# A hybrid decoder block whose POOL opens with a maximum over partitions, and whose norm scale moves behind the first diagonals

## The chip, the cores and the metric

The kernel runs on one core of one Trainium2 chip. The metric is the device time of one execution, in microseconds (us), as the median of several runs; lower is better. The engines are called as the profile calls them: PE (matrix multiplications; PEld is its weight load), DVE (vector), ACT (activations), POOL (general purpose) and SP (here it only issues DMA transfers).

## The reference, cut to what matters

One decoder block over 1024 tokens of width 1024. The input is normalised over its width and multiplied by the norm weight, one wide projection makes all heads and gates, a linear recurrence (HGRN2) and a sliding-window attention run beside each other, and two output projections follow.

```python
def rms_norm(x, w):
    xf = x.astype(jnp.float32)
    xf = xf * lax.rsqrt(jnp.mean(xf * xf, axis=-1, keepdims=True) + EPS)
    return xf.astype(x.dtype) * w
...
xn = rms_norm(x, norm_w[l])
proj = xn @ w_in[l]
hq, hf, hi, hg, aq, ak, av, ag, mh, ma = jnp.split(proj, SPLIT_POINTS, axis=-1)
lb = lb_all[l]
f = lb + (1.0 - lb) * jax.nn.sigmoid(hf.astype(jnp.float32))
...
merged = jax.nn.sigmoid(mh) * y_h + jax.nn.sigmoid(ma) * y_a
x = x + merged @ w_out[l]
return rms_norm(x, final_norm_w)
```

The change touches the first two lines of the second part: the norm, and the first columns of the projection (`hf`).

## The kernel before

Float32 products are made of float16 ones: each operand is scaled by a power of two and split into a high and a low half, and three products (high by high, high by low, low by high) are summed. So each weight block of 1024 by 256 needs its largest absolute value (DVE reduces each partition, POOL takes the maximum over partitions with `all_max`, L119), a power of two made of it (`pow2_of`, L124, four small DVE operations), a high half on ACT (`hi_part`, L193) and a low half on DVE (`lo_part`, L198). The first weight block is loaded and converted in two parts of 128 columns.

The activations go the same way. Tokens come in tiles of 128. For a tile, ACT squares the row and sums it (`square`, L418) and takes the root of the mean plus `eps` (L419); DVE makes the reciprocal root more exact in four steps and writes it into a diagonal matrix `dg` made from the identity `ident` (`diag`, L430 to L445). PE multiplies the tile by the diagonal, which turns and normalises it at once (`turn_x`, L451, into a bank `xT`, one bank for each 128 columns k, tile j filling a quarter of it). When the four tiles of a half are in a bank, ACT writes the high half `xh` with the scale `nws` (`split_x`, L455) and DVE the low half `xl` (L456). `nws` is the norm weight times a power of two, which comes from the largest norm weight (`norm_max`, L341, and `norm_scale`, L346). PE then multiplies `xh` and `xl` by the first weight block (`mm_first`, L1097, into `pf`).

Until the end of L1190 the order on PE, DVE, ACT and POOL is written out by hand, line by line; each engine works through its own list in order. SP issues its transfers in program order. Behind that a scheduler orders the work.

The lists at the start are, before the change. POOL: memsets of `ident`, `ones` and `eps`, the affine select that makes `ident` a unit matrix (in the helper file masks.py), then the maxima over partitions. PE: four transposes of `ident` into a bank that nobody reads (`warm`, L1091), the norm weight turned from 8 rows into 8 columns (`turn_rows`, L147), twenty more `warm`, then the first `turn_x`. DVE: a copy of the turned norm weight, its maximum, the power of two and `nws` as soon as POOL has answered, then the maximum of the first weight part, its power of two, and only then the diagonals. ACT: a first small Sqrt that reads `eps` (`tab`, L1088), the squares of tiles 0 and 1, `hi_part`, the squares of tiles 2 and 3.

## Time and profile before

| what | value |
|---|---|
| time, median of 3 runs | 1214.54 us (1213.32 to 1217.31) |
| the profiled execution's own time | 1214.3 us |
| its span | 1212.5 us |
| PE busy | 1165.0 us, 96% of the span |
| DVE busy | 832.6 us, 69% |
| ACT busy | 546.9 us, 45% |
| POOL busy | 43.9 us, 4% |

A timeline row gives the start, the duration, the engine, the line with the operation, the tiles written and read, the count of instructions merged into the row, and in brackets the idle time of that engine just before and what ended it. "issue" there means that the engine waited for nothing that the profile shows. In the chain of work that ended last, each row is a start, a length and what ran. [...]

### The profile page before, as it was taken

To read this page: it belongs to the slowest core of one execution; us is meant where nothing else is said; L and a number is where in the kernel's file an instruction comes from. 1 tells how busy PE (TensorE), PEld (TensorE's weight loads), DVE (VectorE), ACT (ScalarE), POOL (GpSimd) and SP (SyncE) were. 2 spreads that over 40 slices of the span, in tenths; PEclk is the share of its full clock that TensorE was granted. 3 is DMA by queue.
4 is the path that set the end of the run, shared out by engine and by line. 5 is a ranking of instruction groups with operands and counts; after the bars stand their busy time and mean duration, and the time that the engine had idled before them with its cause. 6 is when DMAs were issued, how large, how long until landed. Compare 5 with 4: busy or idle time off the path is not lost.

```text
span 1212.5 us, 18364 instructions
## 1 busy us (share of the span) xinstructions
PE 1165.0 (96%) x7258; PEld 689.1 (57%) x7258; DVE 832.6 (69%) x1999; ACT 546.9 (45%) x1053; POOL 43.9 (4%) x97
## 2 busy tenths in 40 slices
PE   4999999999999999999999989999897999999997
PEld 3557687687687667675554544445454444444444
DVE  2876955866686778666787774358896877467645
ACT  2733524444353333525864762138677550223323
POOL 0250000000000000000000000000000000000000
PEclk8999999999999999999999999999999999999999
DMA  5121111111111111111453551114455412121312
GB/s 208 36 96 44 35 36 36 35 36 36 35 36 36 35 36 35 36 36 35 108 105 93 113 114 59 55 39 114 106 108 99 111 35 70 35 96 44 139 53 105
DMA packets 132647, 82.48 MB, mean 68 GB/s; under 512 B 81200, under 2 KB 129360, under 8 KB 132560
## 3 DMA queue, kind: packets, MB, share of 16 engines
q1 hardware_dynamic: 132560, 81.30, 24.4%
q8 instruction: 57, 0.93, 0.3%
q14 instruction: 30, 0.25, 0.1%
HBM read 57.17 MB, written 4.19 MB: 51 GB/s over the span
## 4 chain that ended last, share of the span: by engine, by line
PE 77%; DVE 10%; ACT 6%; DMA 5%; issue 2%; SPq 0%; POOL 0%; DVEq 0%; POOLq 0%; ACTq 0%
PE pm L302 19%; PE pg L302 10%; PE pv L314 7%; PE po L1250 7%; PE pq L302 7%; PE paq L302 5%; PE pf L302 5%; PE lv L582 4%; DMA pT<-ph 3%; ACT sp L784 2%; DVE ph L795 2%; PE pk L302 2%; PE pf L1097 1%; DVE sp L774 1%; DMA aot<-ohl 1%
## 5 line engine op out<-in xcount | busy, mean ns | idle before, releaser
L302 PEld LDWEIGHTS <-wh 128*128 128x128 f16 x2304 | 224.3, 98 | 251.4 <-issue 6.2
L302 PEld LDWEIGHTS <-wl 128*128 128x128 f16 x1152 | 112.8, 98 | 129.4
L235 ACT ACTIVATE wh<-raw,p_s 128x512 f16<-128x512 f32 x164 | 104.8, 709 | 119.9 <-issue 42.7
L236 DVE SCALAR_TENSOR_TENSOR wl<-raw,p_s,wh 128x512 f16<-128x512 f32 x164 | 114.2, 749 | 48.5 <-PE pm L302 18.4
L204 DVE TENSOR_REDUCE wmx<-raw 128x1 f32<-128x2048 f32 x45 | 102.7, 2283 | 63.4 <-DMA raw<-in_w_in_dram 42.5
L302 PE MATMUL pm<-hl,wh 128*128 128x512 f16 x512 | 117.0, 379 | 0.0
L1250 PE MATMUL po<-wo,hl 128*128 128x512 f16 (+1 forms) x408 | 83.1, 366 | 0.0
L784 ACT ACTIVATE sp<-sp,anm 128x256 f32<-128x256 f32 (+1 forms) x128 | 61.7, 483 | 25.1 <-DVE anm L779 24.6
L314 PEld LDWEIGHTS <-xh 128*128 128x128 f16 x640 | 62.7, 98 | 7.6
L1250 PEld LDWEIGHTS <-hl 128*128 128x128 f16 x408 | 39.9, 98 | 43.3
L302 PE MATMUL pg<-xh,wh 128*128 128x512 f16 x256 | 60.8, 379 | 0.9 <-DVE qs L731 0.9
L302 PE MATMUL pg<-xl,wh 128*128 128x512 f16 x256 | 61.6, 379 | 0.0
L587 DVE COPY_PREDICATED sc<-lmask,lv 128x512 f32<-128x512 uint8 x56 | 49.5, 886 | 17.6 <-PE lv L582 17.4
L302 PE MATMUL pm<-xh,wh 128*128 128x512 f16 x256 | 61.3, 381 | 0.0
L302 PE MATMUL pm<-xl,wh 128*128 128x512 f16 x256 | 61.3, 379 | 0.0
L302 PE MATMUL pg<-xh,wl 128*128 128x512 f16 x256 | 61.1, 379 | 0.0
L302 PE MATMUL pm<-xh,wl 128*128 128x512 f16 x256 | 60.6, 379 | 0.0
L302 PE MATMUL pm<-hl,wl 128*128 128x512 f16 x256 | 60.5, 379 | 0.0
L582 PEld LDWEIGHTS lv<-kq 128*128 128x128 f32 x448 | 56.6, 192 | 5.0
L582 PE MATMUL lv<-kq 128*128 128x128 f32 x448 | 58.2, 275 | 0.0
L774 DVE CUSTOM_DVE_ANT_0 sp<-as,amask,qsc 128x256 f32<-128x256 f32 (+1 forms) x128 | 52.3, 463 | 4.5 <-DMA pT<-ph 4.2
L567 ACT ACTIVATE kq<-k 128x512 f32<-128x512 f32 x56 | 35.8, 641 | 42.5 <-PE lv L582 37.8
(209 smaller groups left out, 1879.6 us busy)
## 6 DMA issues: line engine op xcount, KB each, us to landing
raw<-in_w_in_dram SPq DMA_DIRECT2D x33, 1024.0 KB, 5.1
xt<-in_x_dram SPq DMA_DIRECT2D x8, 512.0 KB, 6.7
raw<-in_w_branch_hgrn_dram SPq DMA_DIRECT2D x4, 1024.0 KB, 5.2
raw<-in_w_branch_attn_dram SPq DMA_DIRECT2D x4, 1024.0 KB, 5.4
raw<-in_w_out_dram SPq DMA_DIRECT2D x4, 1024.0 KB, 5.1
xr<-in_x_dram SPq DMA_DIRECT2D x8, 512.0 KB, 7.9
out_dram<-xr SPq DMA_DIRECT2D x8, 512.0 KB, 2.6
raw<-in_w_in_dram SPq DMA_DIRECT2D x2, 512.0 KB, 4.1
```

The lines of the kernel that those rows point to most:

```text
L204: V.tensor_reduce(mx[:, j : j + 1], self.raw[:, ks], axis=AX.XY, op=ALU.max, apply_absolute_value=True)
L235: A.activation(hi, raw, AF.Copy, scale=s[:])
L236: V.scalar_tensor_tensor(lo, raw, s[:], hi, ALU.mult, ALU.subtract)
L302: PE.matmul(ps, w[:, k, ci * P : (ci + 1) * P], act(ai, k, t0, HALF), start=(n == 0), stop=(n == 3 * KT - 1))
L314: PE.matmul(ps, act(ai, k, t0, P), w[:, k, n0 : n0 + ncol], start=(n == 0), stop=(n == 3 * KT - 1))
L567: A.activation(view(kq[:, 0], 0, mdims), view(k, 0, kdims), AF.Copy)
L582: PE.matmul(lv[:, ms], kq[:, 0, ms], kq[:, 1, ms], start=True, stop=True)
L587: V.copy_predicated(view(sc, c, qdims), view(lmask[c], 0, mdims), view(lv, 0, mdims))
L774: V.tensor_tensor_reduce(self.s[:, i, 0:nk], self.ps[a][:, e * 256 : e * 256 + nk], amask[:, self.n % 2, 0:nk], qsc[:], NEG, ALU.add, ALU. ...
L784: A.activation(self.s[:, i, 0 : self.nk], self.s[:, i, 0 : self.nk], AF.Exp, bias=self.nm[:, i : i + 1], accum_out=self.dn[:, i : i + 1],)
L795: V.scalar_tensor_tensor(self.hl[:, 1], self.s[:, :, 0 : self.nk], 2.0**14, self.hl[:, 0], ALU.mult, ALU.subtract)
L1250: PE.matmul(ps[:, g[0] : g[1]], mact(ai, k, tb * P, P), w, start=(t == 0), stop=(t == 3 * KT - 1))
```

## The change

Five things are changed.

1. POOL begins with a memset of a new tile `zero` and a maximum over partitions of it, whose result nobody reads. The affine select on `ident`, and the memsets of `ones` and `eps`, come behind it.
2. The norm weight is loaded by ACT's DMA queue in place of SP's, into 8 rows of a tile of 128 rows that DVE has filled with zeros. Its maximum is taken from these rows, before they are turned.
3. On DVE the diagonals of tiles 0 and 1 come ahead of both powers of two. The power of two of the weight part now comes ahead of that of the norm weight; the turned norm weight is copied only there.
4. The 24 `warm` instructions read a tile `wsrc` that DVE fills with ones, and are plain matrix products in place of transposes; the turning of the norm weight comes behind all of them.
5. The diagonal of tile 2 comes ahead of the low half of the weight part's first rows.

```diff
@@ -132,13 +132,19 @@
+    zero = const.tile([P, 1], F32, name="zero")
+    G.memset(zero[:], 0.0)
+    all_max(zero[:])
     ident = const.tile([P, P], F32, name="ident")
     make_identity(nc, ident[:])
...
-    nwr = slot("nwr", [KT, P])
-    SP.dma_start(nwr[:], norm_w[0].rearrange("(k p) -> k p", p=P))
+    nwr = slot("nwr", [P, P])
+    V.memset(nwr[:], 0.0)
+    A.dma_start(nwr[0:KT, :], norm_w[0].rearrange("(k p) -> k p", p=P))
+    wsrc = slot("wsrc", [P, P])
+    V.memset(wsrc[:], 1.0)
...
@@ -340,12 +346,12 @@
     def norm_max():
         nmx = small("nmx", 1)
-        V.tensor_reduce(nmx[:], nw[:], axis=AX.X, op=ALU.max, apply_absolute_value=True)
+        V.tensor_reduce(nmx[:], nwr[:], axis=AX.X, op=ALU.max, apply_absolute_value=True)
         return all_max(nmx[:])
 
-    def norm_scale(top):
+    def norm_scale(top, turned):
         sx, sxi = pow2_of(top, 10)
-        yield
+        V.tensor_copy(nw[:], turned[:, 0:KT])
         V.tensor_copy(sxi_c[:], sxi[:])
         V.tensor_scalar(nws[:], nw[:], sx[:], None, ALU.mult)
 
@@ -1088,9 +1094,7 @@
         for i in range(WARM):
-            PE.transpose(warm[:, 0:P], ident[:], ident[:])
-            if i == 3:
-                V.tensor_copy(nw[:], turn_rows(nwr, KT)[:, 0:KT])
+            PE.matmul(warm[:, 0:P], wsrc[:], wsrc[:], start=True, stop=True)
...
@@ -1111,19 +1115,20 @@
         hf_tiles(0)
         top = norm_max()
-        in_turn(norm_scale(top))
         first.max_part(0)
         tok[0].square(True)
         tok[1].square(True)
+        in_turn(tok[0].diag())
+        turned = turn_rows(nwr[0:KT], KT)
+        in_turn(tok[1].diag())
         first.scale_part(0)
         first.hi_part(0, 0)
-        in_turn(tok[0].diag())
+        norm_scale(top, turned)
         tok[2].square(True)
-        in_turn(tok[1].diag())
+        in_turn(tok[2].diag())
         first.lo_part(0, 0)
         tok[3].square(True)
         first.hi_part(0, 1)
-        in_turn(tok[2].diag())
         in_turn(tok[3].diag())
         first.lo_part(0, 1)
```

POOL's list from its first memset in the kernel's body to its second maximum, before (ISA is an instruction without operands that the program puts in ahead of some operations; `p_r` is the result of a maximum, `nmx` the norm weight's, `wmx` the weight part's):

```order
masks.py:197 MEMSET ident 128x128
L138 MEMSET ones 128x1
L339 MEMSET eps 128x1
masks.py:199 ISA
masks.py:199 AFFINE_SELECT ident<-ident 128x128 [waits Pool_49]
L121 ISA
L121 ISA p_r_197<-nmx_195 128x1 [waits DVE_49]
L121 ISA p_r_210<-wmx_208 128x1 [waits DVE_49]
```

And the same stretch of POOL now, from the memset of `zero`:

```order
L136 MEMSET zero 128x1
masks.py:197 MEMSET ident 128x128
L121 ISA
L121 ISA p_r_75<-zero 128x1 [waits Pool_49]
L141 MEMSET ones 128x1
L345 MEMSET eps 128x1
masks.py:199 AFFINE_SELECT ident<-ident 128x128 [waits Pool_49]
L121 ISA p_r_201<-nmx_199 128x1 [waits DVE_49]
L121 ISA p_r_205<-wmx_203 128x1 [waits DVE_49]
```

The operand-less ISA ahead of the affine select is gone, one ISA ahead of the first maximum is left, and `ones`, `eps` and the affine select stand behind that maximum.

DVE's list from its start to the first low half, before, cut to the rows between the norm weight's reduction and the end of the first diagonal:

```order
L343 TENSOR_REDUCE nmx_195<-nw 128x1 [waits DVE_49]
L128 TENSOR_SCALAR p_r_197<-p_r_197 128x1 [waits Pool_49]
...
L350 TENSOR_SCALAR nws<-nw,p_s_201 128x8 [waits DVE_49]
L175 TENSOR_REDUCE wmx_208<-raw_96 128x1 [waits DMAHW1_49]
L128 TENSOR_SCALAR p_r_210<-p_r_210 128x1 [waits Pool_49]
...
L131 RECIPROCAL p_s_220<-p_inv_219 128x1 [waits DVE_49]
L430 RECIPROCAL xr_101<-xr_101 128x1 [waits Activation_49]
...
L445 TENSOR_SCALAR dg_230<-ident,xr_101 128x128 [waits DVE_49]
```

DVE's list now, from the same reduction to `nws`:

```order
L349 TENSOR_REDUCE nmx_199<-nwr_84 128x1 [waits DMAHW1_49,DVE_49]
L181 TENSOR_REDUCE wmx_203<-raw_103 128x1 [waits DMAHW0_49]
L436 RECIPROCAL xr_108<-xr_108 128x1 [waits Activation_49]
...
L451 TENSOR_SCALAR dg_215<-ident,xr_108 128x128 [waits DVE_49,Pool_49]
L436 RECIPROCAL xr_114<-xr_114 128x1 [waits Activation_49]
...
L451 TENSOR_SCALAR dg_223<-ident,xr_114 128x128 [waits DVE_49]
L128 TENSOR_SCALAR p_r_205<-p_r_205 128x1 [waits Pool_49]
...
L356 TENSOR_SCALAR nws<-nw,p_s_237 128x8 [waits DVE_49]
```

The two reductions stand side by side, two diagonals come ahead of the first operation that reads an answer of POOL, and `nws` has moved behind them.

## Rows read from the trace of the kernel before

**Rows 1.** The page's part 2: busy tenths of PE in 40 slices of 30.3 us

```profile
PE   4999999999999999999999989999897999999997
```

**Rows 2.** Timeline of POOL, 0 to 57 us

```profile
0.97 0.10 POOL L339 MEMSET eps<- 128x1 f32 x1
9.13 0.28 POOL masks.py:199 TENSOR_SCALAR_AFFINE_SELECT ident<-ident 128x128 f32<-128x128 f32 x1 [8.06 <-issue]
18.40 0.38 POOL L121 PARTITION_ALL_REDUCE p_r<-nmx  x1 [8.99 <-issue]
...
52.33 0.35 POOL L121 PARTITION_ALL_REDUCE p_r<-wmx  x1 [23.46 <-DVE wmx L204]
52.55 0.27 POOL L380 MEMSET mk<- 128x128 f32 x1
...
56.10 1.72 POOL L383 TENSOR_SCALAR_AFFINE_SELECT mk<-mk 128x128 f32<-128x128 f32 x1
```

**Rows 3.** The chain that ended last, three of its pieces before the first `pf`

```profile
1.13 8.00 issue
...
11.20 7.20 issue
...
23.08 7.96 PE xT L451 x48
```

**Rows 4.** Timeline of ACT, 6 to 31 us

```profile
6.96 1.06 ACT L418 ACTIVATE xj<-xt 128x1024 f32<-128x1024 f32 x1 [4.67 <-DMA xt<-in_x_dram]
...
8.14 0.29 ACT L419 ACTIVATE xr<-xm,eps 128x1 f32<-128x1 f32 x1
8.34 1.04 ACT L418 ACTIVATE xj<-xt 128x1024 f32<-128x1024 f32 x1
...
22.17 0.72 ACT L193 ACTIVATE wh<-raw,p_s 128x512 f16<-128x512 f32 x1 [12.37 <-DVE p_s L131]
22.80 1.04 ACT L418 ACTIVATE xj<-xt 128x1024 f32<-128x1024 f32 x1
...
29.96 3.57 ACT L455 ACTIVATE xh<-xT,nws 128x512 f16<-128x512 f32 x6 [3.73 <-PE xT L451]
```

**Rows 5.** Timeline of DVE, 19 to 25 us

```profile
19.71 1.21 DVE L175 TENSOR_REDUCE wmx<-raw 128x1 f32<-128x1024 f32 x1
...
21.41 0.15 DVE L128 TENSOR_SCALAR p_r<-p_r 128x1 f32<-128x1 f32 x1 [0.49 <-POOL p_r L121]
...
22.05 0.14 DVE L430 RECIPROCAL xr<-xr 128x1 f32<-128x1 f32 x1
...
22.73 0.29 DVE L445 TENSOR_SCALAR dg<-ident,xr 128x128 f32<-128x128 f32 x1
22.93 0.16 DVE L430 RECIPROCAL xr<-xr 128x1 f32<-128x1 f32 x1
...
23.83 0.74 DVE L198 SCALAR_TENSOR_TENSOR wl<-raw,p_s,wh 128x512 f16<-128x512 f32 x1
24.49 0.16 DVE L430 RECIPROCAL xr<-xr 128x1 f32<-128x1 f32 x1
```

**Rows 6.** Timeline of PE, 10 to 39 us

```profile
10.72 4.16 PE L1091 MATMUL warm<-ident 128*128 128x128 f32 x20
...
36.44 1.89 PE L1097 MATMUL pf<-xh,wh 128*128 128x512 f16 x8
38.17 1.89 PE L1097 MATMUL pf<-xl,wh 128*128 128x512 f16 x8
```

**Rows 7.** Windows of the whole core: start, PE, PEld, DVE, ACT, POOL, clock, DMA

```profile
17.80:18.00 0.20, 0.00 (x0) 0.00 (x0) 0.00 (x0) 0.00 (x0) 0.00 (x0) 0.50 1.13 358
...
27.50:28.00 0.50, 0.50 (x4) 0.50 (x4) 0.50 (x1) 0.00 (x0) 0.00 (x0) 0.50 0.00 0
28.00:28.20 0.20, 0.20 (x4) 0.20 (x4) 0.20 (x1) 0.00 (x0) 0.00 (x0) 0.97 0.00 0
```

**Rows 8.** Timeline of SP, then the answer on tile `xt`, 0 to 60 us

```profile
1.75 2.20 SPq L410 DMA_DIRECT2D xt<-in_x_dram  x4
...
DMA to landing us min/median/max: 5.2/6.7/9.4
```

## The prediction

> **What bounds the kernel now.** I read the busy digits first. PE is at 9 tenths or more in nearly every slice except the first, where it has 4 of 10 [rows 1]. So after some 31 us the kernel is as long as PE's work, and an earlier start of that work moves the end by about as much; a change that only touches the first 31 us is priced by when the first `xh` is written, 29.96 us [rows 4], since `pf` and all later products follow it.

> Next I read the chain of waits back from there. Two of its pieces are time in which nothing that the profile shows was waited for: 8.00 us from 1.13, and 7.20 us from 11.20 [rows 3]. POOL's timeline says where they lie: POOL stands 8.06 us ahead of its first affine select, then 8.99 us ahead of its first maximum over partitions [rows 2]. Later operations of both kinds do not pay it: the maximum at 52.33 ends a wait on DVE, and the affine select at 56.10, after several maxima, follows work without such a pause [rows 2]. The lists show an ISA instruction ahead of each of the two first uses, and none later. I read both pauses as the price of making code for these operations ready, once for each ISA.

> The third thing is PE at the diagonals: 24 products (48 records) take 7.96 us [rows 3]. The clock was at 0.50 until 28.0 and full after [rows 7]; PE had been idle since 14.88 (10.72 + 4.16) [rows 6], and the clock was down by 17.8 [rows 7]. Of the 7.96 us, 4.92 lie at half clock and 3.04 at full. If a product takes twice as long at half clock, it is (4.92/2 + 3.04)/24 = 0.23 us at full and 0.46 at half.

> **The change, part by part.** *One pause in place of two.* The new list has one ISA. POOL's pause starts at 1.07 as before (0.97 + 0.10 [rows 2]). Its length is bounded by the two rows: 8.06 (the place at the start, the other code) and 8.99 (the code that stays, a later place with transfers running). I take 8.5, the middle, since each row shares one property with the new pause. The maximum over `zero` then starts at 1.07 + 8.5 = 9.6. The next POOL operation follows a maximum after 0.22 us (52.33 to 52.55 [rows 2]); `ones` and `eps` are two short memsets, `eps` 0.10 us, so `eps` is ready at about 9.95, and the affine select (0.28) is done at about 10.3.

> [...]

> *A new wait on ACT.* The first small Sqrt reads `eps`, and the squares of all tiles are queued behind it. Before, the square of tile 0 ran at 6.96, when its data came [rows 4]. Now it waits for `eps`: 9.95 plus 0.03 and one short ACT operation (0.2), 10.2. This is the hidden price, 3.2 us, since the diagonals were not what counted before; now they are.

> *The chain from there,* all by rows. Square to the end of its root: 6.96 to 8.43 is 1.47 [rows 4]. Diagonal: 22.05 to 23.02 is 0.97, and DVE takes the next operation 0.88 after the start [rows 5]. So root 0 ends at 11.67, diagonal 0 at 12.67, and the first turn starts at 12.7 (before: 23.08 [rows 3]). The second square follows 1.38 after the first (6.96 to 8.34 [rows 4]): 11.58, root at 13.05, diagonal from 13.08, DVE free at 13.96. Now the power of two of the weight part: from its first operation to `hi_part` 0.76 (21.41 to 22.17 [rows 4, 5]), so `hi_part` at 14.72. Behind it on ACT, tile 2's square 0.63 later (22.17 to 22.80 [rows 4]): 15.35, root 16.82. Diagonal 2 from 16.85, done 17.82, DVE free 17.73; the low half takes 0.66 of DVE (23.83 to 24.49 [rows 5]): 18.39. Tile 3's square starts at 16.73 and its root ends at 18.20, so it is DVE that is late: diagonal 3 from 18.4, done 19.37. One turn later, with 0.1 us of handing over, the first bank is full, and `xh` starts at 19.37 + 0.33 + 0.1 = 19.8. The norm weight's power of two, the copy and `nws` fill DVE after 14.7 (seven small operations, some 1.2 us at the spacing of rows 5), while ACT squares tile 2: nothing.

> That is 29.96 - 19.8 = 10.2 us at the first `xh`. With a pause of 8.06 it is 10.6, with 8.99 it is 9.7. It is less than the 17 us of pauses: one pause stays, the squares have moved behind it, and PE's half-clock turns, no longer the bound, give back a part.

> *What is late next.* Before, DVE's reduction of the second weight part ended ahead of the first `xh`; now DVE reaches it only after diagonal 3 and a low half (19.3 + 0.7 + 1.2 = 21.2, against `xh` at 19.8). POOL's answer and the power of two come about 1 us later relative to `xh`, and ACT's next `hi_part` stalls for a few tenths. I charge 0.2.

> *The rest at nothing.* The reduction over 128 rows in place of 8 columns costs DVE less than the 1.21 us of 1024 columns [rows 5]; both reductions run while POOL pauses. The norm weight's transfer is issued on ACT's queue at about 1.2. No row shows a transfer on that queue; the tiles' land 5.2 to 9.4 us after issue [rows 8], so at worst it lands at 10.6, and the two reductions behind it (under 0.3 and 1.21) free DVE at 12.1, 0.4 later than diagonal 0 could start. I take 0 with 0.4 for the range. SP has one issue less ahead of the weights. Tiles 2 and 3 are issued by 3.95 and landed by 13.4 at the slowest [rows 8], ahead of 15.35. The 24 `warm` products run from about 1.3 and take 24 x 0.23 = 5.5 to 24 x 0.46 = 11.0 us, so they end between 6.8 and 12.3, under the wait for diagonal 0. A few rows of the scheduled part change places with neighbours; I take nothing.

> **PE's clock** is the unknown. With `warm` over by then, PE may idle for up to 6 us ahead of the first turn. Then the clock is low for the turns of tiles 0 and 1 (2 x 6 x 0.46 = 5.5 us from 12.7, to 18.2), which still ends about when diagonal 2 comes (17.8): no loss, and PE has then worked without a break as it had before the rise at 28.0 [rows 7]. If the clock is still high, these turns end at 15.5, PE idles to 17.8, and the clock may fall just there; then the turns of tiles 2 and 3 take 5.5 in place of 2.8 us. I add 0.4 for this in the forecast.

> [...]

> The sum: 1214.3 - 10.2 + 0.2 + 0.4 = 1204.7; the profiled execution stands 0.2 under the median of the runs shown, so I set 1204.8.

> **The rivals.** *The clock falls before the products.* Then the turns lose up to 2.7 us, and `pf` products at half clock take 0.43 for 0.22 us (8 from 36.44 to 38.17 [rows 6]), a few of them before it rises: 1 us. The gain is about 7: 1207.5. For it: PE's gaps in the new order. Against: after 18 us PE has work almost without pause.

> *The first pause is not the affine select's.* If the 8.06 us are POOL's start and only the 8.99 us the maximum's, the new list pays 17 us ahead of the maximum over `zero`, `eps` comes at 18.5, `xh` at 28.4, and the gain is 1.5: 1212.8. For it: the affine select is POOL's first operation that is no memset. Against: an ISA stands ahead of each pause, and only one is left.

> *The slower one: the code changes back.* If the affine select on `ident` and the maxima cannot share their code, POOL pays three times: maximum over `zero` at 9.1, affine select at 9.5 + 8.1 = 17.6, the norm weight's maximum at 17.9 + 9.0 = 26.9, the weight part's at 27.2, `hi_part` at 28.4. From `hi_part` to `xh` the sum above has 5.1, so `xh` is at 33.5 and the time 1217.8. It turns slower from the third pause on. Against: the affine select at 56.10 after maxima paid nothing [rows 2].

> **How the numbers follow.** Forecast 0.70 (1204.8; 1203 to 1206 by the pause's ends), clock 0.20 (1207.5), start-up pause 0.07 (1212.8), slower 0.03 (1217.8). A measurement of this kernel tells about 0.3%, 3.6 us, from no change. Faster holds the first two, 0.90; same 0.07; slower 0.03. The range leaves the last two out: from 1202.5 (pause at 8.06, no clock loss, runs 1 us apart) to 1208.5 (clock lost, pause at 8.99).

> **What would show it.** One pause on POOL, 8 to 9 us, ahead of the first maximum; squares of tiles 0 and 1 right behind `eps` at about 10; first turn near 12.7, first `xh` near 19.8; granted clock full where `pf` starts. A second pause on POOL, or a low clock beyond 20 us, would make it wrong.

## The result

| | kernel before | changed kernel |
|---|---|---|
| time, median of 6 runs each | 1215.36 us (1213.32 to 1217.31) | 1202.99 us (1199.13 to 1204.39) |
| the profiled execution, its time and span | 1214.3, 1212.5 us | 1204.39, 1202.6 us |

The ratio is 0.9895, with a 95% interval of 0.9875 to 0.9914: 12.4 us less, between 10.5 and 15.2. The forecast was 1204.8 with a range of 1202.5 to 1208.5. The profiled execution of the changed kernel is the slowest of its six runs and 9.9 us faster than the one before, so what follows accounts for 9.9, and says where the other executions differ.

The page of the changed kernel, PE's busy digits and its clock in 40 slices. PE's first slice has gone from 4 tenths [rows 1] to 9; the rest reads as before.

```profile
PE   9999999999999999999999989999897999999997
PEclk9999999999999999999999999999998999999999
```

POOL's timeline of the changed kernel is the surprise. The forecast had one pause of 8.5 us where there had been two, of 8.06 and 8.99 [rows 2]. There is none: the maximum over `zero` runs at 1.17, 0.14 us after the memset of `ident` ends (0.83 + 0.20).

```profile
0.83 0.20 POOL masks.py:197 MEMSET ident<- 128x128 f32 x1
1.17 0.35 POOL L121 PARTITION_ALL_REDUCE p_r<-zero  x1
1.39 0.16 POOL L141 MEMSET ones<- 128x1 f32 x1
1.42 0.16 POOL L345 MEMSET eps<- 128x1 f32 x1
1.47 0.35 POOL masks.py:199 TENSOR_SCALAR_AFFINE_SELECT ident<-ident 128x128 f32<-128x128 f32 x1
3.97 0.35 POOL L121 PARTITION_ALL_REDUCE p_r<-nmx  x1 [2.14 <-DVE nmx L349]
6.14 0.35 POOL L121 PARTITION_ALL_REDUCE p_r<-wmx  x1 [1.82 <-DVE wmx L181]
```

ACT's timeline of the changed kernel answers to [rows 4]. With `eps` there at 1.58, the squares wait for their data alone: tile 0 at 6.08, tile 1 at 8.19 for another transfer. `hi_part` runs at 11.36 in place of 22.17, the first `xh` at 17.12 in place of 29.96.

```profile
6.08 1.06 ACT L424 ACTIVATE xj<-xt 128x1024 f32<-128x1024 f32 x1 [2.88 <-DMA xt<-in_x_dram]
...
8.19 1.06 ACT L424 ACTIVATE xj<-xt 128x1024 f32<-128x1024 f32 x1 [0.63 <-DMA xt<-in_x_dram]
...
11.36 0.72 ACT L199 ACTIVATE wh<-raw,p_s 128x512 f16<-128x512 f32 x1 [1.69 <-DVE p_r L128]
...
17.12 3.58 ACT L461 ACTIVATE xh<-xT,nws 128x512 f16<-128x512 f32 x6 [1.70 <-PE xT L457]
```

PE's timeline of the changed kernel has a wait that the forecast did not see: after five turns (10 records) PE stands for 1.67 us until the copy `nw` on DVE. A turn is one product of a tile with its diagonal, and the sixth needs the bank that the copy reads.

```profile
1.26 7.67 PE L1097 MATMUL warm<-wsrc 128*128 128x128 f32 x48 [1.26 <-DVE wsrc L147]
8.86 0.22 PE L155 MATMUL vT<-ident,nwr 8*128 8x8 f32 x1
9.02 1.38 PE L457 MATMUL xT<-dg,xt 128*128 128x128 f32 x10
12.06 6.14 PE L457 MATMUL xT<-dg,xt 128*128 128x128 f32 x38 [1.67 <-DVE nw L354]
```

PE's clock (the granted share of full speed) falls behind this wait (0.51 from 12.4 to 13, 0.50 to 15.8), and PE's turns are then what the first `xh` waits for: it starts 1.1 us after the last diagonal is done on DVE (16.02, the row below). In the run after_again, a second profiled execution of the same kernel without this fall (1.00 in each window from 10 to 18), it starts 0.57 after it (15.64 to 16.21). So of the 17.12 some 0.5 are PE's.

```profile
15.74 0.28 DVE L451 TENSOR_SCALAR dg<-ident,xr 128x128 f32<-128x128 f32 x1
```

**Where the time went.** The first `xh` is 12.84 us earlier, the span only 9.9. To see what happens between, I cut every profiled execution at the first `xh` on ACT and at three marks on POOL: the maxima behind the two branches (`bmx`) and the one behind the last of the two halves (`mmx`). POOL's timeline of the changed kernel has them here; in the kernel before the same three stand at 536.86, 981.21 and 1124.94.

```profile
525.60 0.35 POOL L121 PARTITION_ALL_REDUCE p_r<-bmx  x1 [52.58 <-DVE bmx L905]
971.40 0.35 POOL L121 PARTITION_ALL_REDUCE p_r<-bmx  x1 [74.28 <-DVE bmx L905]
...
1115.13 0.35 POOL L121 PARTITION_ALL_REDUCE p_r<-mmx  x1 [19.65 <-DVE mmx L974]
```

| stretch, us | before | changed | difference |
|---|---|---|---|
| start to first `xh` | 29.96 | 17.12 | -12.84 |
| first `xh` to first `bmx` | 506.90 | 508.48 | +1.58 |
| first to second `bmx` | 444.35 | 445.80 | +1.45 |
| second `bmx` to last `mmx` | 143.73 | 143.73 | 0.00 |
| last `mmx` to the end | 87.56 | 87.47 | -0.09 |

The 1.58 are the clock. Windows of PE in the changed kernel (start and end, length, busy time and count, granted clock, DMA share, GB/s) show it at 0.58 and 0.57 from 36 to 40, behind the gaps in PE's work around the second half's first `xh`; `pf` products start 0.43 us apart at 37 and 0.22 at 40:

```profile
34.00:36.00 2.00, 1.02 (x6) 1.00 0.00 0
36.00:38.00 2.00, 1.53 (x4) 0.58 0.00 0
38.00:40.00 2.00, 2.00 (x9) 0.57 0.00 0
40.00:42.00 2.00, 2.00 (x15) 1.00 0.03 8
```

This fall is a matter of the single execution: another profiled execution of the same kernel (the run after_again, below) has none, and 506.91 in that stretch. All fourteen profiled executions of this document divide so: the nine without a fall there took 506.88 to 506.91, the five with one 508.35 to 508.59. The 1.45 lie in the attention, and their cause is not settled; it comes up again below.

### The profile page after: what moved, and what is told of

Read it like the earlier page. It is cut to its first block, busy times and chain, and to the rows that moved or that the text cites. A ratio compares the mean times of both kernels' runs of the same rounds, so it can differ in the third digit from the quotient of the medians.

```text
span 1202.6 us, 18417 instructions
## 1 busy us (share of the span) xinstructions
PE 1171.1 (97%) x7282; PEld 692.5 (58%) x7282; DVE 832.1 (69%) x2001; ACT 547.0 (45%) x1053; POOL 45.8 (4%) x99
## 4 chain that ended last, share of the span: by engine, by line
PE 81%; DVE 8%; DMA 6%; ACT 4%; issue 1%; SPq 0%; DVEq 0%; ACTq 0%
PE pm L308 19%; PE pg L308 13%; PE pv L320 8%; PE po L1255 7%; PE pq L308 7%; PE pf L308 5%; PE paq L308 5%; PE lv L588 4%; DMA pT<-ph 2%; PE pk L308 2%; PE pf L1101 2%; ACT sp L790 1%; DVE ph L801 1%; DMA aot<-ohl 1%; PE rb L664 1%; PE op L643 1%
## 5 line engine op out<-in xcount | busy, mean ns | idle before, releaser
L593 DVE COPY_PREDICATED sc<-lmask,lv 128x512 f32<-128x512 uint8 x56 | 49.4, 885 | 17.6 <-PE lv L588 17.4
L121 POOL PARTITION_ALL_REDUCE p_r<-wmx x47 | 20.9, 450 | 885.8 <-DVE wmx L210 687.0
```

Source lines behind the costliest of these rows:

```text
L121: last_all_max[0] = G.partition_all_reduce(r[:], mx, channels=P, reduce_op=bass_isa.ReduceOp.max)
L593: V.copy_predicated(view(sc, c, qdims), view(lmask[c], 0, mdims), view(lv, 0, mdims))
```

## The experiments

The theory after the result, **A**, is a reading of the pauses: an ISA takes 8 to 10 us when POOL has the code of other operations, as after the affine select in the kernel before, and nothing when it has the right one; the maxima's code also carries the affine select, and it was still there from the execution before. By A the kernel before changes the code twice in every execution, for the affine select (8.06) and back (8.99). "Code" is the forecast's word for what an ISA changes; no row shows what POOL does in a pause. Its rival, **B**: the maxima's code is free at every start, and only the affine select's own ISA had a price.

**The other code at the end.** The changed kernel with one addition on POOL behind its last maximum, for which the list has a new ISA; and as its control an affine select in the same place, for which it has none.

```diff
         if n == 1:
             converts(n_out + 4)
+            oth = small("oth", 1)
+            G.tensor_tensor(oth[:], seq[n_out + 3][0].wscale_inv[:], ones[:], ALU.add)
```

> The changed kernel with one addition of a 128x1 tile on POOL behind its last maximum, some 70 us before the end; the list has a new ISA ahead of it, so POOL's code changes there. Theory A (the code of the maxima was still there from the execution before, so the one ISA at the start cost nothing, where the kernel before changed the code twice in every execution): now the start has a pause of 8 to 9 us ahead of the maximum over zero, eps comes at 10, the first xh at about 20 in place of 17.1, and the time is 2 to 4 us above the changed kernel's 1203.0. Theory B (the maxima's code is free at every start, whatever ran before; only the affine select's own ISA had a price): no pause, first xh at 17.1, 1203.

> The control for the run with the addition: in the same place an affine select of a 128x1 tile, for which the list has no ISA. Theories A and B both: no pause at the start, first xh at 17.1, 1203. A pause here would mean that any late work on POOL brings it back, and both would fall.

With the addition the time is 1206.52 us (ratio to before 0.9942, 0.9926 to 0.9958), with the control 1202.77 (0.9910, 0.9895 to 0.9925). POOL's timeline with the addition:

```profile
0.81 0.20 POOL masks.py:197 MEMSET ident<- 128x128 f32 x1
11.58 0.38 POOL L121 PARTITION_ALL_REDUCE p_r<-zero  x1 [10.56 <-issue]
11.84 0.16 POOL L141 MEMSET ones<- 128x1 f32 x1
11.87 0.16 POOL L345 MEMSET eps<- 128x1 f32 x1
...
1126.01 0.18 POOL L1247 TENSOR_TENSOR oth<-p_inv,ones 128x1 f32<-128x1 f32 x1 [6.99 <-DVE hl L984]
```

And with the control:

```profile
0.83 0.20 POOL masks.py:197 MEMSET ident<- 128x128 f32 x1
1.17 0.35 POOL L121 PARTITION_ALL_REDUCE p_r<-zero  x1
```

With one small operation 80 us before the end, the maximum over `zero` stands behind a pause of 10.56 us; with the control in its place there is none. B falls, and A fits: the list at the start is the same in both, and the two differ in what POOL runs last. One reading beside A stays open: that a program which never changes its code has it in place from the start, whatever ran before. A program that changes the code in its middle and ends with the maxima's would tell the two apart; none was run. The addition itself, at 1126.01, is off the path. Its row puts a wait of 6.99 us down to DVE's `hl`, which the addition does not read, so how much of this is the change of code is not told.

This run also tests the forecast's sum, since it has the one pause that the forecast assumed. ACT's timeline with the addition has the wait on `eps` that was foreseen, and the first `xh` at 21.93:

```profile
12.06 0.20 ACT L1094 ACTIVATE tab<-eps 128x1 f32<-128x1 f32 x1 [9.09 <-POOL eps L345]
12.17 1.04 ACT L424 ACTIVATE xj<-xt 128x1024 f32<-128x1024 f32 x1
...
21.93 3.58 ACT L461 ACTIVATE xh<-xT,nws 128x512 f16<-128x512 f32 x6 [1.18 <-PE xT L457]
```

The sum gave 19.8 for a pause of 8.5; with 10.56 it gives 21.86, and the forecast of the time becomes 1206.9 for the 1206.52 measured. From the pause on, the working was right to 0.1 us at the first `xh`. Inside it two small errors cancel: the last diagonal was done 0.1 earlier than worked out, and from there to `xh` it took 0.58 in place of 0.43.

**Which part carries the gain.** Part 1 alone on the kernel before, and the changed kernel without part 1:

```diff
+    zero = const.tile([P, 1], F32, name="zero")
+    G.memset(zero[:], 0.0)
+    all_max(zero[:])
     ident = const.tile([P, P], F32, name="ident")
     make_identity(nc, ident[:])
```

> The kernel before with part 1 alone (the maximum over a zero tile first, the affine select behind it). Theory A with the pauses as all of the gain: no pause, squares of tiles 0 and 1 at 6.5 and 8.5, hi_part right behind them at about 9.8 as POOL has answered by then, first xh at 14.5 to 15.5, so as fast as the changed kernel or 2 us faster: 1201 to 1203. Rival (the new order of diagonals and scales is needed for the gain): first xh at 17 or later, time 1205 or more.

> The changed kernel without part 1: no maximum over a zero tile, POOL's list at the start as before, all else as changed. Theory A: both pauses come back, the answers of POOL at 18.8 and 19.0, hi_part at 19.8, first xh at about 25, 8 us later than in the changed kernel: 1210 to 1211. Rival (the new order makes the gain): 1203 to 1205.

Part 1 alone: 1198.39 us (ratio 0.9879, 0.9865 to 0.9894), faster than the whole change, and than the 1201 to 1203 that I had expected. Without part 1: 1214.66 us, ratio 1.0008 (0.9999 to 1.0018), no gain at all; I had expected 1210 to 1211. POOL's timeline without part 1 has both pauses, the first 2 us longer than in the kernel before:

```profile
11.12 0.28 POOL masks.py:199 TENSOR_SCALAR_AFFINE_SELECT ident<-ident 128x128 f32<-128x128 f32 x1 [10.05 <-issue]
20.13 0.38 POOL L121 PARTITION_ALL_REDUCE p_r<-nmx  x1 [8.72 <-issue]
```

PE's timeline without part 1 shows the second half of the miss. The diagonals of tiles 0 and 1 were early, but after five turns PE waited 8.07 us for the copy `nw`, which now stands behind POOL's answers:

```profile
11.78 2.50 PE L454 MATMUL xT<-dg,xt 128*128 128x128 f32 x10
22.35 5.94 PE L454 MATMUL xT<-dg,xt 128*128 128x128 f32 x38 [8.07 <-DVE nw L351]
```

In the profiled execution, the fastest of ten, the first `xh` came at 27.21, 2.75 ahead of the kernel before, and the stretch between the two `bmx` took 446.11 in place of 444.35, 1.76 more.

In part 1 alone `hi_part` runs at 9.59 and the first `xh` at 15.57; the changed kernel has 11.36 and 17.12. So part 3, which puts the scales behind the diagonals, is itself a wait once POOL answers early. DVE's list holds the scale, ready since 6.5, behind the diagonal of tile 1, whose root ends at 9.66. Theory **C** says so; it was tested by moving the scales back, and by moving only the copy.

**The scales ahead of the diagonals.**

```diff
+        first.scale_part(0)
+        first.hi_part(0, 0)
         in_turn(tok[0].diag())
         turned = turn_rows(nwr[0:KT], KT)
+        norm_scale(top, turned)
         in_turn(tok[1].diag())
-        first.scale_part(0)
-        first.hi_part(0, 0)
-        norm_scale(top, turned)
         tok[2].square(True)
```

> The changed kernel with the power of two of the weight part, and hi_part, ahead of the diagonals of tiles 0 and 1, and the norm weight's scale and copy between them. Theory C (with the pauses gone POOL has answered by 6.5, so part 3 of the change, which puts these scales on DVE behind the diagonal of tile 1, is itself a wait: hi_part ran at 11.4 and could run at 9.7): hi_part at 9.7, the copy done by 9.5 so that PE's bank is free, first xh at 14.9, 2.2 us earlier than 17.1, time 1200.5 to 1201. Rival (the squares' own data bound the start, the order of the scales doesn't matter): first xh at 16.5 to 17, time 1203.

Measured: 1200.92 us (ratio 0.9884, 0.9869 to 0.9899). ACT's timeline has `hi_part` at 9.22 and the first `xh` at 14.45, 2.7 ahead of the changed kernel's 17.12 and 1.8 ahead of its 16.21 in after_again. C stands for the start.

```profile
9.22 0.71 ACT L199 ACTIVATE wh<-raw,p_s 128x512 f16<-128x512 f32 x1
...
14.45 3.58 ACT L461 ACTIVATE xh<-xT,nws 128x512 f16<-128x512 f32 x6 [1.18 <-PE xT L457]
```

**The copy alone.** One line moved: the copy of the turned norm weight between the diagonals.

```diff
-        V.tensor_copy(nw[:], turned[:, 0:KT])
...
         turned = turn_rows(nwr[0:KT], KT)
+        V.tensor_copy(nw[:], turned[:, 0:KT])
         in_turn(tok[1].diag())
```

> The changed kernel with one line moved: the copy of the turned norm weight stands between the diagonals of tiles 0 and 1 in place of behind the powers of two. It frees the bank that PE's sixth turn needs at about 9.3 in place of 12.0. Theory C: PE's wait of 1.7 us goes, PE's clock does not fall at 12.4, the first xh follows diagonal 3 (16.0) at 16.5, 0.6 earlier; time 1202.4, not to be told from 1203. Rival (the clock falls anyway): first xh at 17.

Measured: 1203.27 us (0.9905, 0.9888 to 0.9921), first `xh` at 16.91. PE's wait on `nw` is gone, and its clock did not fall (1.00 in every window to 60), yet PE then waits for diagonal 2. DVE's timeline has the copy in its new place (first row), PE's the wait:

```profile
9.93 0.17 DVE L1122 COPY nw<-vT 128x8 f32<-128x8 f32 x1 [1.17 <-PE vT L155]
...
9.82 2.94 PE L456 MATMUL xT<-dg,xt 128*128 128x128 f32 x24
14.82 3.16 PE L456 MATMUL xT<-dg,xt 128*128 128x128 f32 x24 [2.06 <-DVE dg L450]
```

The gain is 0.2 of the expected 0.6. The copy now waits on DVE for the turned norm weight, which PE makes only behind all its warm products (9.7 in this execution, 8.9 in the changed kernel's), and holds diagonal 1 and `hi_part` with it: 11.66 in place of 11.36. The bank and the fall of the clock had held the first `xh` up by some 0.5 us, the rest of the 1.67 being covered by the diagonals behind `hi_part`; 0.3 of these 0.5 come back as the new wait.

**The warming.** Part 1 alone with 44 warm transposes, so that PE works until the first diagonal; and the changed kernel with one warm product.

```diff
-WARM = 24
+WARM = 44
```

```diff
-WARM = 24
+WARM = 1
```

> The kernel before with part 1 alone and 44 warm transposes in place of 24, so that PE works until about 9, when the first diagonal comes. In part 1 alone the turns ran at half clock from 9.4 and the first xh came at 15.6, though diagonal 3 was done at about 14. If the clock is what is late there: no fall of the clock, first xh at 14.5, time 1197.5. If not: first xh at 15.5 and 1198.4.

> The changed kernel with one warm product in place of 24: what part 4 is worth. If the warming matters: the turns of tile 0 run at half clock from 9.0 in place of full, first xh at 17.5 or later, time 1203.5 or more. If PE's turns wait for the bank and for diagonals 2 and 3 anyway: first xh at 17.1, time 1203.

With 44: 1200.49 us (0.9883, 0.9866 to 0.9900). The first `xh` came at 14.31, as expected of the clock, but the clock fell later, as in the changed kernel (0.80, 0.50 and 0.84 in the windows from 32 to 38; 508.35 to the first `bmx`), and the attention took 447.27: not faster. Nor do the 44 get the credit for the start: the second execution of part 1 alone, below, has 14.59 with 24 of them, and its turns at the full pace (24 records in 2.97 us). With one: 1202.05 (0.9899, 0.9874 to 0.9924), the first `xh` at 16.20, as in after_again (16.21), though the 48 records of turns took 8.23 us. In the changed order the diagonals hide the slow turns, and part 4 is worth nothing that can be measured.

**The same once more, on one chip.** Four kernels with five rounds: the changed kernel, part 1 alone, the scales first, and the scales first with one warm product (the two edits above).

> The changed kernel once more, beside the next three on the same chip, as their measure: 1203, first xh at 17.

> The kernel before with part 1 alone, once more. If parts 2 to 5 cost what the first xh says (15.6 against 17.1): 1.5 us below the changed kernel, 1201.5. If the 1198.4 of the first measurement stands: 4 below. If only the clock's phase made it: the same as the changed kernel.

> The changed kernel with the scales ahead of the diagonals, once more: first xh at 14.5, 2.6 us ahead of the changed kernel, so 1200.4 by theory C; the same as the changed kernel if the start is given back later.

> The changed kernel with the scales ahead of the diagonals and one warm product in place of 24. If the warming is worth something once the turns are what is late: they run at half clock from 9.5, 24 products at up to 0.46 us, first xh at 16 to 17 in place of 14.5, and the time 1.5 to 2.5 us above the run with 24. If PE's clock is of no account there: 14.5 and the same time.

| kernel | median (range), us | ratio to before (95%) | first `xh` | to first `bmx` | to second `bmx` |
|---|---|---|---|---|---|
| changed | 1202.79 (1202.39 to 1204.56) | 0.9905 (0.9890 to 0.9920) | 16.21 | 506.91 | 446.72 |
| part 1 alone | 1198.38 (1198.05 to 1199.44) | 0.9869 (0.9852 to 0.9885) | 14.59 | 506.91 | 443.58 |
| scales first | 1202.54 (1201.13 to 1204.25) | 0.9901 (0.9886 to 0.9916) | 15.03 | 508.59 | 447.65 |
| scales first, one warm | 1201.24 (1200.15 to 1203.16) | 0.9891 (0.9876 to 0.9906) | 16.07 | 508.39 | 445.72 |

Part 1 alone beats both kernels: 1198.4 twice, 4.4 us below the changed kernel on the same chip, with runs that do not overlap. In the profiled executions its start explains 1.6 (14.59 against 16.21) and the attention 3.1 (443.58 against 446.72) of 4.8 us between the spans. The scales first gain 1.2 at the first `xh` here, but the profiled execution, the slowest of its four, loses it in the two later stretches, and the medians are the same (1202.54 and 1202.79). So a faster start did not show as a faster kernel; the expected 1200.4 missed. The first `xh` moved by 1.0 with the warming (15.03 against 16.07), where the turns are what is late; the medians, with overlapping ranges, do not show it, where 1.5 to 2.5 us were expected.

**What stays open.** Between the two `bmx`, the kernel before and part 1 alone took 444.35, 443.06 and 443.58; ten of the eleven other profiled executions, with another order of parts 2 to 5 or with 44 warm transposes, took 444.96 to 447.65. There the scheduler's list on PE differs in a few places, where part 1 alone has that of the kernel before. But the changed kernel with one warm product, which has the changed kernel's order on PE there, took 443.65, so that the same order is seen with anything from 443.65 to 446.72. The clock's mean does not decide it: from 535 to 985 it was 0.985 in part 1 alone, with 443.06, and 0.986 in the changed kernel, with 445.80. Nor do PE's waits on the transposed probabilities (`pT`): 11.4 us before, 7.7 in the changed kernel, 8.6 and 9.5 in part 1 alone. Whether the list, the places of the clock's falls or the transfers set these 2 to 3 us was not settled.

## Why the prediction was right, and where it was not

*The bound* was right: the kernel is PE's work behind the first `xh`. From the second `bmx` on, the two kernels differ by 0.1 us, and the 12.84 us of the start come through but for the 3.0 in the table.

Of the five signs that the forecast named, only the last came, the full clock where `pf` starts (1.00 from 16 to 20). There was no pause, and the squares (6.08), the first turn (9.02) and the first `xh` (17.12) were all earlier than said. One of its two signs of being wrong, a low clock beyond 20 us, came in the profiled execution, at 36 (0.58).

*One pause in place of two* was wrong, and it is the term that was mis-sized: 8.5 us taken, 0 measured (1.17 for 9.6). I read each of the two pauses as the price of an ISA. The rows of before could not show an ISA that costs nothing, because the kernel before ends with the code that it needs second, and so, by theory A, finds the wrong one at every start. The lower bound of 8.06 was a bound from rows that did not cover the case. The run with the addition and its control have the same ISA in the same place, and the pause there was 10.56 us in the one and 0 in the other.

*The wait of ACT on `eps`*, 3.2 us, fell with the pause: `eps` came at 1.58. It was there in the run with the addition, where `tab` started 0.03 us after `eps` (12.03 to 12.06) and the square at 12.17.

*The chain behind it* was right by that run (21.93 against 21.86), but for its last step: the 0.33 us from the last diagonal to the full bank is neither of the two costs of a product that the forecast had worked out, and the step took 0.58 for 0.43. In the changed kernel other things were late in its place: the transfer of tile 1 (8.19), then the scale behind diagonal 1, which the forecast had walked through without asking what it would cost if POOL answered early, and at the end PE's turns.

*The bank* was missed: the sixth turn waits for the copy `nw`. It cost 1.67 us of PE, 0.5 of it at the first `xh` together with the clock that fell behind it, and 8.07 us of PE where POOL was late.

*The clock* was right in kind and wrong in place. It fell at 12.4 (0.54), behind the wait on the bank, was back by 15.8 (0.93), and did not touch `pf`; then it fell at 36 (0.58), where the forecast had not looked, and cost 1.58 there. The forecast had charged 0.4, for the turns.

*The scheduled part*, taken at nothing, is +1.45 in the profiled pair, with the cause open.

The errors cancel in part: -2.7 at the first `xh` (17.12 for 19.8) and some 2.4 given back later (3.0, where 0.6 was charged), so the profiled execution's 1204.39 is close to the forecast's 1204.8 by luck; the median of the six runs is 1202.99, and the two fastest of them, 1199.13 and 1201.74, have the highest mean clocks, 0.996 and 0.995 for 0.990 to 0.992 in the others. The sum's own last step was off by 0.1 as well: 1204.7 and 0.2 make 1204.9. Of the rivals, the start-up pause and the third change of code fell with the pauses, and the run with the clock lost ahead of `pf` did not occur.

## What to carry to other kernels

Before pricing an ISA on POOL, ask what the program runs last there: here the eleven profiled executions of kernels that open with a maximum, and run no other ISA's operations behind it, had no pause at the start, and the three others had one of 8.06 to 10.56 us. When a long wait goes, look again at each reordering that was made to hide it; here the reordering held the scale back, and part 1 alone was 4.4 us faster, some 1.6 of them by its start. And compare executions by marks at fixed places of the program: so a gain at the start is told from what a later stretch adds by itself.

## What the runs showed of the hardware

The clock record did not tell PE's pace ahead of its first fall. In the changed kernel it reads 1.00 from the start, but the records of warm products start 0.21 us apart between 3 and 4 and 0.11 apart between 6 and 7, twice the pace. Windows of PE, with columns as above (a window also counts the records that reach into it):

```profile
3.00:4.00 1.00, 1.00 (x7) 1.00 0.87 252
...
6.00:7.00 1.00, 1.00 (x12) 1.00 0.99 406
```

So a 1.00 in the first microseconds did not tell the pace; the count of records in a window did, 7 against 12.
